# Pairing a head's backward retention scan with the next head's forward scan, with early chunks held in DRAM

## The chip, the core and the metric

The kernel runs on one core of a Trainium2 chip. The core has five engines that work side by side, each through its own queue in a fixed order: TensorE (PE in the profile; its weight loads are PEld) for matrix products and transposes, VectorE (DVE), ScalarE (ACT), GpSimd (POOL), and SyncE (SP), which here only issues DMA transfers. Engines wait for one another by semaphores. SBUF is the on-chip memory, PSUM the eight banks in which TensorE leaves its products, and DRAM the memory outside. The metric is the device time of one launch in microseconds; the times named before are the median of three runs.

## The reference

One block of a bidirectional encoder on 1024 tokens and 16 learned meta tokens that are put ahead of them, with 1024 channels, in float32. A normalised stream goes through one wide projection; two branches read parts of it, retention and windowed attention, and both are gated, projected and merged. The change concerns the retention branch and, through the order of work, the attention behind it.

```python
def _retention_direction(q, k, v, log_gamma, strict):
    ...
    decay = jnp.where(vis[None], jnp.exp(jnp.where(vis, rel, 0.0)[None] * log_gamma[:, None, None]), 0.0)
    s = jnp.einsum("bnihd,bnjhd->bnhij", q, k) * decay[None, None]
    inner = jnp.einsum("bnhij,bnjhv->bnihv", s, v)
    k_decay = jnp.exp((CHUNK - 1 - idx)[:, None] * log_gamma[None, :])
    kv = jnp.einsum("bnjhd,bnjhv->bnhdv", k * k_decay[None, None, :, :, None], v)
    chunk_decay = jnp.exp(CHUNK * log_gamma)[None, :, None, None]

    def step(state, kv_c):
        return chunk_decay * state + kv_c, state

    _, s_prev = lax.scan(step, jnp.zeros((B, H, DK, DV), jnp.float32), jnp.moveaxis(kv, 1, 0))
    ...
    cross = jnp.einsum("bnihd,bnhdv->bnihv", q * q_decay[None, None, :, :, None], s_prev)
    return (inner + cross).reshape(B, L, H, DV)

def _bidirectional_retention(q, k, v, log_gamma_f, log_gamma_b):
    fwd = _retention_direction(q, k, v, log_gamma_f, False)
    flip = lambda t: jnp.flip(t, axis=1)
    bwd = flip(_retention_direction(flip(q), flip(k), flip(v), log_gamma_b, True))
    return fwd + bwd
```

There are four retention heads of key size 128 and value size 256, and eight chunks of 128 tokens, with a short chunk 0 for the meta tokens. The sum of the two directions is normalised over each head's 256 values before it goes on. Attention has eight heads in two groups; each block of 128 queries sees itself, its two neighbours and the meta keys, with a sink logit in the softmax.

## The kernel before

Each float32 product is made of three float32r matmuls (`mm3`, lines 69 to 71): the operands are split into a rounded high part and the rest, and high times high, low times high and high times low are added up. The high part is made by a copy on ScalarE or GpSimd (`pool_hi`, line 74), the low part by a subtraction on VectorE (`dve_lo`, line 77). So every operand that changes costs two small instructions on other engines, ahead of the matmul.

PSUM has eight banks in four tags: three for projections (`pj`), two for transposes and scores (`p1`), two for state increments and attention scores (`p2`), and one (`p3`) for the output products of both scans and of attention.

The stages, in the order of time: a start, in which the first projection and the row norms are made; retention, head by head, from about 33 us; the values of attention (`gen_av`, tile `pav`); attention by four pairs of heads, from about 357 us; and from about 589 us the gates and the three big products, which the diff leaves alone.

`retention(h, fill)` treats one head. Its forward part runs over chunks 0 to 8. `stage1(c)` projects the values of chunk c (`pv`), transposes the keys and makes the scores in one bank (`tr`, lines 466 and 468), scales the keys for both directions (`kh`, `kl`) and applies the decay table to the scores (`sd`). `stage2(c)` makes the inner and the cross product in the `p3` bank (`pa`), adds both into the output chunk `op` (lines 506 and 507), makes the state increments of both directions (`pkv`), updates the forward state (`Sf`) and splits it, and keeps the backward increment in `kvb` (line 523). All eight `op` and all seven `kvb` stay in SBUF until the backward part needs them.

The backward part runs over chunks 8 to 1. For each it updates the state (`Sb`, line 572) and splits it, makes the cross product in `p3` (`pb`), adds it to `op` (line 579), takes mean and variance (lines 583 to 585), normalises the chunk before (line 587) and, for the chunk two before, transposes it (`finish`, `to`, line 555), copies it to `ost` with a scale (line 560), and stores two chunks at a time to `oTr_d`. The last two chunks of a head are finished inside the next head's forward part (`pend`).

Between the steps of the backward part, `fill(KT)` takes a portion of a generator of other projections, eight groups of matmuls: queries and keys of the next retention head (`gen_qk`, tiles `pk` and `pq`) for heads 0 to 2, and for head 3 attention's keys (`gen_ak`, `pak`), half the first pair's queries (`gen_aq`, `paq`) and one gate (`gen_gate(7)`, `pgt`). A projection of queries is 24 matmuls of 512 columns a tile and is evacuated by two VectorE products (`rope_evac`, lines 159 and 160) and two adding transfers of GpSimd. The order in the queues is set when the program is built: a scheduler places instructions by their priority and readiness, `issue_after` ties some behind others, and it draws filler ahead where the main work is not ready. So the built queues need not stand in the order of the source.

Attention of a pair (`attention(hp, fill)`) has three stages for each block n: scores of two heads (`ps`), mask and maximum in one VectorE instruction (line 1203), exponential, and a scaling on GpSimd; transposes of the probabilities (`pt`) with their splits (`pal`, `pbl`, `pm`); and the product with the values (`po`, in `p3`). `FILL` gives the portions of filler behind each block: for pair 0 the second half of its own queries, then the first half of the next pair's, and so on. Beside pair 0, `sums_of_x` loads x in 16 tiles (`xs`, line 664), scales them on ScalarE (line 669), subtracts them on VectorE (line 671) and stores the differences, which the big products use later.

Of the kernel before, what the change touches and what calls it, by code (L numbers as in the profile page):

```python
# [14 lines left out]
NM = 16  # L15
# [23 lines left out]
def block_kernel(ctx: ExitStack, tc: tile.TileContext, xT, x, w_in, w_rb, w_ab, w_out, vecs, dec, sink,  # L39
# [22 lines left out]

    xs_d = {n: dram.tile([4, P, 512], F32, tag=f"xs{n}", name=f"xs{n}") for n in ("T1", "T2", "T3", "T4")}
# [104 lines left out]
    tabt = ra.tile([P, 3 * P + 5], F32, name="tabt")  # L168
    idx = tabt[:, 3 * P:3 * P + 5]
    mask = ra.tile([P, MW], F32, name="mask")  # L170
# [44 lines left out]
    def decay_table(hs):  # L215
        for h in hs:
            t = ra.tile([P, P], F32, tag="dd", bufs=2, name=f"dd{h}")
            nc.vector.tensor_scalar(t, tabt[:, 2 * P:3 * P], lg[:, 4 + h:5 + h], None, op0=ALU.mult)
            nc.vector.scalar_tensor_tensor(t, tabt[:, P:2 * P], lg[:, h:h + 1], t, op0=ALU.mult, op1=ALU.add)
            nc.scalar.activation(DT[:, h], t, AF.Exp)  # L220
# [17 lines left out]
    with tc.tile_pool(name="setup", bufs=1, reuse_waits="tile") as st:  # L238
# [35 lines left out]
        nc.sync.dma_start(tabt[:, 0:3 * P], tab[:, MW:MW + 3 * P])  # L274
# [155 lines left out]
    pend = []  # L430

    def retention(h, fill):
        q, kt = qk[h]
        qh, ql = [], []
        for i in range(2):
            a = rp.tile([P, 512], R, tag="qh", bufs=2, name=f"qh{h}_{i}")
            b = rp.tile([P, 512], R, tag="ql", bufs=2, name=f"ql{h}_{i}")
# [5 lines left out]
        vmeta = rp.tile([NM, 256], F32, tag="vmeta", bufs=2, name=f"vmeta{h}")  # L443
        st1 = {}
        state = {"f": None, "b": None}
        pins = []

        def qs(ts, c):
            return ts[(c - 1) // 4][:, P * ((c - 1) % 4):P * ((c - 1) % 4) + P]
# [8 lines left out]
        def stage1(c):  # L458
            n = NM if c == 0 else P
            pv = first.pop(0) if first else projT(wv, c, f"pv{h}_{c}", vmeta)  # L460
            vh = rp.tile([P, 256], R, tag="vh", bufs=4, name=f"vh{h}_{c}")
            vl = rp.tile([P, 256], R, tag="vl", bufs=4, name=f"vl{h}_{c}")
            state["v"] = nc.scalar.copy(vh[0:n], pv[0:n, 0:256]).ins
# [27 lines left out]
        def split_state(sr_, nm):  # L491
            a = rp.tile([P, 256], R, tag="Sh", bufs=2, name=f"Sh{nm}")
            b = rp.tile([P, 256], R, tag="Sl", bufs=2, name=f"Sl{nm}")
            state["S"] = pool_hi(a, sr_)
            dve_lo(b, sr_, a)
            return a, b

        def stage2(c):
            n, vh, vl, kd, s = st1.pop(c)
            if c > 0:  # L500
# [4 lines left out]
                o = op[c - 1]  # L505
                nc.scalar.activation(o, pa[:, 0:256], AF.Copy, scale=rcol[:, c:c + 1])
                nc.vector.scalar_tensor_tensor(o, pa[:, 256:512], qdf(h, c), o, op0=ALU.mult, op1=ALU.add)
            if kd:
                pk = p2(f"pkv{h}_{c}")
            if "f" in kd:  # L510
                a, b = kd["f"]
                mm3(pk[:, 0:256], a[0:n], b[0:n], vh[0:n], vl[0:n], True, True)
                new = rp.tile([P, 256], F32, tag="S", bufs=2, name=f"Sf{h}_{c}")
                if c == 0:
                    nc.vector.tensor_copy(new, pk[:, 0:256])
                else:
                    nc.vector.scalar_tensor_tensor(new, state["f"], cdf(h), pk[:, 0:256], op0=ALU.mult, op1=ALU.add)
# [11 lines left out]
        for c in range(9):  # L529
            if c < 8:  # L530
                stage1(c + 1)
            if c == 1:
                while pend:
                    pend.pop(0)()
# [893 lines left out]
```

## Time and profile before

| | |
|---|---|
| median of 3 runs | 1093.3 us (1090.18 to 1094.16) |
| the profiled execution | 1094.51 us, of it 1092.7 us span |
| mean granted TensorE clock | 0.995 |
| DRAM read, written | 105.89 MB, 52.43 MB |
| idle time of TensorE in the span | 1092.7 - 1068.1 = 24.6 us |

The page of the profile gives the busy time of each engine; the span in 40 slices; the DMA queues; the chain of work that ended last, followed back from the end; the costliest groups of instructions with the idle time before them; and the DMA issues. Besides, the trace can be asked for the busy time of each engine in chosen stretches of time (with the clock granted to TensorE, DMA share and GB/s), for the groups in such a stretch, and for the single instructions in order of time. Matmuls overlap in TensorE's pipeline, so that the duration of one in a row (about 0.28 us for 256 columns) is longer than the distance to the next.

### The profile page before, as it was taken

The numbers are of one execution on the slowest core, as the hardware profiler recorded it, in microseconds if no ns is written. First come the engines' busy times: TensorE is split into PE (matmuls) and PEld (weight loads), VectorE is DVE, ScalarE is ACT, GpSimd is POOL, SyncE is SP. The second block draws the span as 40 slices with busy tenths as digits, with TensorE's granted clock in tenths as the row PEclk, the third lists the DMA queues.
The fourth block names the chain that finished last, engine by engine and source line by source line (L and its number), as shares of the span: only waits on it lengthen the run. The fifth ranks groups of instructions, "written<-read, shape, count | busy, mean of one in ns | idle before, by whom it ended". The sixth has DMA issues, their size and how long they took to land.

```text
span 1092.7 us, 17365 instructions
## 1 busy us (share of the span) xinstructions
PE 1068.1 (98%) x5975; PEld 922.5 (84%) x5975; DVE 827.4 (76%) x1816; ACT 490.0 (45%) x1132; POOL 265.7 (24%) x394
## 2 busy tenths in 40 slices
PE   8999999999999999999999999999999999999996
PEld 7899999998989889888887778888888788787885
DVE  7785767867946977777557875988889899767765
ACT  7241432413314455635657544454456546433442
POOL 3444334343422555464220000000000000010032
PEclk9999999998999999999999999999999999999999
DMA  7333122231324994243115654779874655789363
GB/s 288 78 86 71 58 42 78 68 69 39 88 59 162 313 269 120 64 98 87 49 40 192 222 204 142 243 246 321 263 285 141 218 201 198 235 209 335 112 115 78
DMA packets 83480, 168.95 MB, mean 155 GB/s; under 512 B 9664, under 2 KB 24512, under 8 KB 82624
## 3 DMA queue, kind: packets, MB, share of 16 engines
q1 hardware_dynamic: 71824, 151.78, 40.5%
q0 software_dynamic: 11136, 15.79, 9.7%
q8 instruction: 47, 0.77, 0.3%
q14 instruction: 41, 0.34, 0.1%
q10 hardware_dynamic: 432, 0.28, 0.1%
HBM read 105.89 MB, written 52.43 MB: 145 GB/s over the span
## 4 chain that ended last, share of the span: by engine, by line
PE 86%; DVE 6%; DMA 4%; ACT 2%; issue 2%; POOL 0%; SPq 0%; DVEq 0%; POOLq 0%; ACTq 0%
PE bz L70 6%; PE bz L71 6%; PE bz L69 6%; PE pv L69 3%; PE paq L70 3%; PE paq L71 3%; PE paq L69 3%; PE pv L70 3%; PE pv L71 3%; PE bo L70 2%; PE bo L69 2%; PE bo L71 2%; PE br L70 2%; PE br L71 2%; PE br L69 2%; PE ba L70 2%
## 5 line engine op out<-in xcount | busy, mean ns | idle before, releaser
L1054 POOL DMA_DIRECT2D mx_d<-c1a x4 | 3.5, 883 | 397.3 <-DVE c1a L1045 397.3
L70 PE MATMUL bz<-big,llz 128*128 128x512 f32 x208 | 82.4, 396 | 0.2 <-DVE llz L77 0.2
L69 PE MATMUL bz<-big,lhz 128*128 128x512 f32 x208 | 81.2, 396 | 0.6 <-ACT lhz L775 0.6
L71 PE MATMUL bz<-big,lhz 128*128 128x512 f32 x208 | 81.7, 394 | 0.0
L69 PE MATMUL pv<-wh,big 128*128 128x256 f32 x256 | 73.4, 287 | 0.7 <-DVE m_qk L160 0.7
L70 PE MATMUL pv<-wh,big 128*128 128x256 f32 x256 | 73.1, 286 | 0.0
L71 PE MATMUL pv<-wl,big 128*128 128x256 f32 x256 | 73.1, 285 | 0.0
L69 PE MATMUL bz<-T,lhz 128*128 128x512 f32 x156 | 61.7, 396 | 0.5 <-ACT u2z L850 0.5
L70 PE MATMUL bz<-T,llz 128*128 128x512 f32 x156 | 61.5, 394 | 0.0
L71 PE MATMUL bz<-T,lhz 128*128 128x512 f32 x156 | 61.4, 394 | 0.0
L1217 POOL TENSOR_SCALAR p<-p,den 128x400 f32<-128x400 f32 (+1 forms) x60 | 44.3, 897 | 43.5 <-DVE den L1211 29.1
L70 PE MATMUL paq<-big,wl 128*128 128x512 f32 x128 | 51.2, 400 | 0.0
L69 PE MATMUL paq<-big,wh 128*128 128x512 f32 x128 | 50.7, 396 | 0.0
L71 PE MATMUL paq<-big,wh 128*128 128x512 f32 x128 | 50.5, 395 | 0.0
L69 PEld LDWEIGHTS pv<-wh,big 128*128 128x128 f32 x256 | 48.9, 191 | 1.1 <-DVE m_qk L160 1.0
L74 POOL TENSOR_SCALAR wh<-wr 128x1024 fp32r<-128x1024 f32 x32 | 39.9, 1335 | 36.8 <-PE pav L70 12.7
L70 PEld LDWEIGHTS pv<-wh,big 128*128 128x128 f32 x256 | 48.8, 190 | 0.1
L71 PEld LDWEIGHTS pv<-wl,big 128*128 128x128 f32 x256 | 48.8, 191 | 0.0
L77 DVE TENSOR_TENSOR wl<-wr,wh 128x1024 fp32r<-128x1024 f32 x34 | 42.9, 1265 | 6.9 <-POOL wh L74 6.9
L69 PEld LDWEIGHTS bz<-big,lhz 128*128 128x128 f32 x208 | 39.0, 188 | 10.7 <-ACT lhz L775 1.5
L70 PEld LDWEIGHTS bz<-big,llz 128*128 128x128 f32 x208 | 39.1, 188 | 9.4 <-DVE llz L77 0.4
L71 PEld LDWEIGHTS bz<-big,lhz 128*128 128x128 f32 x208 | 39.1, 188 | 9.0
(614 smaller groups left out, 3669.2 us busy)
## 6 DMA issues: line engine op xcount, KB each, us to landing
wr<-in_w_in_dram SPq DMA_DIRECT2D x35, 512.0 KB, 4.2
wrz<-in_w_in_dram SPq DMA_DIRECT2D x28, 512.0 KB, 5.4
tg<-tg_d SPq DMA_DIRECT2D x32, 256.0 KB, 5.3
T<-preT SPq DMA_DIRECT2D x6, 1024.0 KB, 7.5
oTr_d<-ost SPq DMA_DIRECT2D x16, 256.0 KB, 2.1
aq<-m_aq POOLq DMA_DIRECT2D x32, 128.0 KB, 4.2
xs<-in_xT_dram SPq DMA_DIRECT2D x16, 256.0 KB, 5.6
xsT<-xs SPq DMA_DIRECT2D x16, 256.0 KB, 5.2
```

Of the source, the lines that this page charges most:

```text
L69: nc.tensor.matmul(o, ah, bh, start=first, stop=False, **kw)
L70: nc.tensor.matmul(o, al, bh, start=False, stop=False, **kw)
L71: return nc.tensor.matmul(o, ah, bl, start=False, stop=last, **kw).ins
L74: return nc.gpsimd.tensor_scalar(o, i, 1.0, 1.0, op0=ALU.mult, op1=ALU.mult).ins
L77: return nc.vector.tensor_tensor(o, i, hi.bitcast(F32), ALU.subtract).ins
L1054: nc.gpsimd.dma_start(d, to, accum_op=ALU.add)
L1217: nc.gpsimd.tensor_scalar(pt[e_][:, 0:wid], pt[e_][:, 0:wid], den[:, e_:e_ + 1], 1.0, op0=ALU.mult, op1=ALU.mult)
```

## The change

The two parts of a head become two generators, `forward(h)` and `backward(h)`, each of which gives up control after every chunk. A loop over five rounds runs the forward chunks of head h, the backward chunks of head h-1 and a portion of filler in turn. Chunks 1 to 5 (`LATE = 6`) of the forward output and increments 2 to 5 go to two sets of DRAM tiles, `op_d` and `kv_d`, right after they are made; the backward part loads them back two chunks ahead into `opl` and `kvl`, with two buffers each. Chunks 6 to 8 stay in SBUF. So that both scans fit, other buffers are cut: `m1` 4 to 3, `vh` and `vl` 4 to 3, `ost` and `vmeta` 2 to 1, `dd` joins the tag of `rw`, and the forward state is updated in place in one buffer; the split queries get four buffers where they had two, and the split states get tags of their own for each direction.

Beside that, the V weights of head h+1 are loaded in round h's seventh step, the fillers of the last rounds are shuffled (both halves of the first pair's queries, then the keys; the gate goes to attention's pair 0), the rope tables are scaled in round 2, the identity is loaded straight from DRAM, and the mask lies in attention's pool and is loaded when retention's pool is closed, ahead of the loads of x. Numbers of matmuls, transposes and other engine instructions stay as they were, but for three small VectorE instructions less; SP issues 73 more transfers.

```diff
+    op_d, kv_d = ([dram.tile([NB, P, 256], F32, tag=f"{n}{i}", name=f"{n}_d{i}") for i in range(2)] for n in ("op", "kv"))
...
-        m1 = ra.tile([P, 512], F32, tag="m1", bufs=4, name=f"m1_{nm}")
+        m1 = ra.tile([P, 512], F32, tag="m1", bufs=3, name=f"m1_{nm}")
...
+        nc.sync.dma_start(ident, tab[:, MW:MW + P])
+        nc.sync.dma_start(tabt[:, 0:2 * P], tab[:, MW + P:MW + 3 * P])
...
-    nc.vector.tensor_copy(ident, tabt[:, 0:P])
     nc.sync.dma_start(sinkc, sink.partition_broadcast(P))
-    nc.sync.dma_start(mask, tab[:, 0:MW])
...
-    def retention(h, fill):
+    scans = {}
+    LATE = 6
...
+    def split_state(sr_, nm):
+        a = rp.tile([P, 256], R, tag="Sh" + nm[0], bufs=2, name=f"Sh{nm}")
+        b = rp.tile([P, 256], R, tag="Sl" + nm[0], bufs=2, name=f"Sl{nm}")
...
+    def forward(h):
...
-        wv = wv0 if h == 0 else load_w(w_in, U_V + h)
-        kvb = [None] + [rp.tile([P, 256], F32, tag="kvb", bufs=NB - 1, name=f"kvb{h}_{c}") for c in range(1, NB)]
-        op = [rp.tile([P, 256], F32, tag="op", bufs=NB, name=f"op{h}_{c}") for c in range(NB)]
+        kvb, op = {}, {}
+        scans[h] = qh, ql, kvb, op
+        wv = wvs.pop(h)
...
-                o = op[c - 1]
+                kept = c >= LATE
+                o = op[c] = rp.tile([P, 256], F32, tag=f"op{int(kept)}", bufs=2 + kept, name=f"op{h}_{c}")
                 nc.scalar.activation(o, pa[:, 0:256], AF.Copy, scale=rcol[:, c:c + 1])
                 nc.vector.scalar_tensor_tensor(o, pa[:, 256:512], qdf(h, c), o, op0=ALU.mult, op1=ALU.add)
+                if not kept:
+                    nc.sync.dma_start(op_d[h % 2][c - 1], o)
...
-                nc.scalar.copy(kvb[c - 1], pk[:, 256:512])
+                kept = c >= LATE
+                t = kvb[c] = rp.tile([P, 256], F32, tag=f"kvb{int(kept)}", bufs=2 + kept, name=f"kvb{h}_{c}")
+                nc.scalar.copy(t, pk[:, 256:512])
+                if not kept:
+                    nc.sync.dma_start(kv_d[h % 2][c - 1], t)
...
             stage2(c)
-
-
+            yield
+
+    def backward(h):
+
+        qh, ql, kvb, op = scans.pop(h)
...
-                ost[0] = rp.tile([P, 2, 256], F32, tag="ost", bufs=2, name=f"ost{h}_{c}")
+                ost[0] = rp.tile([P, 2, 256], F32, tag="ost", bufs=1, name=f"ost{h}_{c}")
...
         for c in range(NB, 0, -1):
-            o = op[c - 1]
+            if 2 < c <= LATE + 1:
+                l = op[c - 2] = rp.tile([P, 256], F32, tag="opl", bufs=2, name=f"opl{h}_{c}")
+                nc.sync.dma_start(l, op_d[h % 2][c - 3])
+                if c > 3:
+                    l = kvb[c - 2] = rp.tile([P, 256], F32, tag="kvl", bufs=2, name=f"kvl{h}_{c}")
+                    nc.sync.dma_start(l, kv_d[h % 2][c - 3])
+            o = op[c]
...
-            if c < 8:
-                with ExitStack() as behind:
-                    for p in pins:
-                        behind.enter_context(tc.issue_after(p))
-                    fill(KT)
             if c < NB - 1:
                 finish(c + 2)
+            yield
         state["n", 1]()
-        pend.extend([lambda: finish(2), lambda: finish(1)])
+        finish(2)
+        finish(1)
+        yield
...
-    for h in range(NH):
-        fill, drain = filler([*([gen_qk(h + 1)] if h < 3 else [gen_ak(0), gen_aq(0, 0), gen_gate(7)])])
...
-        with tc.issue_after(rotated):
-            retention(h, fill)
+    wvs = {0: wv0}
+    with tc.issue_after(rotated):
+        for h in range(NH + 1):
+            fill, drain = filler([gen_qk(h + 1)] if h < 3 else [gen_aq(0, 0), gen_aq(0, 1)] if h == 3 else [gen_ak(0)])
+            f, b = forward(h) if h < NH else iter(()), backward(h - 1) if h else iter(())
+            for i in range(NB + 1):
+                next(f, None)
+                next(b, None)
+                fill(KT)
+                if h == 2 and i > 6:
+                    turn_factors(*PIECES[2 * i - 14])
+                    turn_factors(*PIECES[2 * i - 13])
+                if h < 3 and i == 6:
+                    wvs[h + 1] = load_w(w_in, U_V + h + 1)
             drain()
-    while pend:
-        pend.pop(0)()
+            for _ in b:
+                pass
...
+    mask = ap.tile([P, MW], F32, name="mask")
+    nc.sync.dma_start(mask, tab[:, 0:MW])
...
-        l = [gen_aq(hp, 1)]
+        l = [gen_aq(hp, 1)] if hp else [gen_gate(7)]
```

More of the change, by code (lines that the diff above doesn't have):

```diff
@@ L460, in stage1 @@
             pv = first.pop(0) if first else projT(wv, c, f"pv{h}_{c}", vmeta)
[L461 to L463 removed]
+            vh = rp.tile([P, 256], R, tag="vh", bufs=3, name=f"vh{h}_{c}")
+            vl = rp.tile([P, 256], R, tag="vl", bufs=3, name=f"vl{h}_{c}")
+            nc.scalar.copy(vh[0:n], pv[0:n, 0:256])
             state["vl"] = dve_lo(vl[0:n], pv[0:n, 0:256], vh[0:n])
@@ L511, in stage2 @@
                 a, b = kd["f"]
+                new = state["f"]
                 mm3(pk[:, 0:256], a[0:n], b[0:n], vh[0:n], vl[0:n], True, True)
-                new = rp.tile([P, 256], F32, tag="S", bufs=2, name=f"Sf{h}_{c}")
                 if c == 0:
+                    new = rp.tile([P, 256], F32, tag="S", bufs=1, name=f"Sf{h}")
                     nc.vector.tensor_copy(new, pk[:, 0:256])
                 else:
-                    nc.vector.scalar_tensor_tensor(new, state["f"], cdf(h), pk[:, 0:256], op0=ALU.mult, op1=ALU.add)
+                    nc.vector.scalar_tensor_tensor(new, new, cdf(h), pk[:, 0:256], op0=ALU.mult, op1=ALU.add)
                 state["f"] = new
@@ L531, in retention @@
                 stage1(c + 1)
-            if c == 1:
-                while pend:
-                    pend.pop(0)()
-            if h == 0 and c == 4:
-                pins.extend((state["v"], state["vl"], state["S"]))
-            if h == NH - 1 and 1 < c < 6:
-                with tc.issue_after(state["vl"]):
-                    turn_factors(*PIECES[c - 2])
             if h < NH - 1 and c == 4:
```

56 lines of the change are left out of this document (23 added, 33 removed).

## The prediction, made before the changed kernel ran

> **What bounds the kernel now.** I read the page first: its busy table, its clock row and its chain of waits.
>
> ```profile
> span 1092.7 us, 17365 instructions
> PE 1068.1 (98%) x5975; PEld 922.5 (84%) x5975; DVE 827.4 (76%) x1816; ACT 490.0 (45%) x1132; POOL 265.7 (24%) x394
> PEclk9999999998999999999999999999999999999999
> PE 86%; DVE 6%; DMA 4%; ACT 2%; issue 2%; POOL 0%; SPq 0%; DVEq 0%; POOLq 0%; ACTq 0%
> ```
>
> TensorE is busy for 98% of the span and carries 86% of the chain. The change issues exactly the matmuls and transposes of before, so it can only win time in which TensorE idles (24.6 us in the span) or runs slowly, and the clock row has one dip, in the tenth slice. The next view, busy time by stretches, was cut at the stages: heads 0 to 3 of retention from 36 to 340 us, and attention's first two head pairs from 357 to 462. Columns: stretch, length, busy time (instructions) of PE, PEld, DVE, ACT and POOL, granted clock, DMA share, GB/s.
>
> ```profile
> 36.00:100.00 64.00, 63.87 (x489) 60.95 (x490) 43.74 (x113) 17.48 (x50) 33.15 (x41) 1.00 0.33 70
> 100.00:175.00 75.00, 74.16 (x572) 70.46 (x571) 56.77 (x159) 25.68 (x80) 31.20 (x47) 1.00 0.28 70
> 175.00:250.00 75.00, 73.98 (x575) 70.73 (x574) 54.59 (x149) 23.43 (x71) 29.36 (x45) 1.00 0.24 58
> 250.00:276.00 26.00, 23.41 (x167) 22.09 (x167) 20.01 (x59) 10.38 (x32) 8.48 (x13) 0.87 0.16 57
> 276.00:340.00 64.00, 64.00 (x406) 57.33 (x405) 44.64 (x113) 16.91 (x49) 24.43 (x35) 1.00 0.31 84
> 357.00:462.00 105.00, 104.44 (x637) 93.34 (x635) 83.98 (x227) 55.99 (x165) 54.12 (x87) 1.00 0.65 192
> ```
>
> Retention is already dense: over the first five stretches TensorE idles 0.13 + 0.84 + 1.02 + 2.59 + 0 = 4.6 us. The idle time stands where one head's backward scan ends and the next head's forward scan begins, and the worst turn, from head 2 to 3, looks like this (timeline of TensorE, the bracket is idle time before the row and its releaser; then the same place in stretches of 2 us):
>
> ```profile
> 256.77 0.36 PE L69 MATMUL pb<-Shb,qh 128*128 128x256 f32 x1 [0.45 <-DVE op L579]
> 258.42 0.41 PE L555 MATMUL to<-ident,op 128*128 128x128 f32 x2 [1.05 <-DVE op L587]
> 259.54 0.48 PE L466 MATMUL tr<-ident,kr 128*128 128x128 f32 x1 [0.61 <-ACT ost L560]
> ...
> 256.00:258.00 2.00, 0.92 (x6) 0.50 (x4) 1.69 (x6) 0.63 (x2) 0.66 (x2) 1.00 0.42 139
> 258.00:260.00 2.00, 0.97 (x5) 0.72 (x6) 1.97 (x7) 0.86 (x3) 1.04 (x3) 0.80 0.00 0
> 260.00:262.00 2.00, 2.00 (x10) 1.55 (x8) 1.62 (x6) 0.74 (x2) 0.27 (x2) 0.50 0.39 131
> 264.00:266.00 2.00, 2.00 (x11) 2.00 (x11) 1.36 (x5) 0.51 (x2) 0.40 (x1) 0.50 0.00 0
> ```
>
> The last chunks have no filler left: scan product, VectorE update, norm, transpose and ScalarE copy follow one another. After about 4 us at under half load the granted clock falls to 0.50 for some 6 us. Over the 26 us the clock is 0.87, which costs 26 x 0.13 = 3.4 us.
>
> **The change part by part.** (1) *Interleaving.* Head h-1's backward chunk stands beside head h's forward chunk and a filler portion, so the turns have other work. If all of it is won: 4.6 + 3.4 = **-8.0 us**. A gain beyond that could lie only in bubbles inside rows counted as busy; zero would remain if the stalls just moved. I take -8.0, since the built program's TensorE queue shows projection matmuls between the scan products at every turn.
>
> (2) *Early chunks through DRAM.* Per head, five forward outputs and four state increments are stored and read back: 18 transfers a head, 72 in all, of 128 KB. The nearest rows, and those of the backward recurrence (transfers: KB, us to landing; then groups of instructions from 36 to 340 us: busy us, mean ns, idle time before):
>
> ```profile
> oTr_d<-ost SPq DMA_DIRECT2D x16, 256.0 KB, 2.1
> ...
> L583 DVE BATCH_NORM_STATS2 bs<-op 128x6 f32<-128x256 f32 x31 | 13.0, 420 | 0.3
> L579 DVE SCALAR_TENSOR_TENSOR op<-pb,qd,op 128x256 f32<-128x256 f32 x27 | 13.0, 481 | 18.4 <-PE pb L71 18.0
> L587 DVE TENSOR_SCALAR op<-op,mv,rs 128x256 f32<-128x256 f32 x30 | 12.6, 418 | 0.2
> L584 DVE BATCH_NORM_AGGREGATE mv<-bs 128x2 f32<-128x6 f32 x31 | 5.4, 173 | 0.3
> L585 DVE TENSOR_SCALAR rs<-mv 128x1 f32<-128x1 f32 x31 | 4.7, 150 | 0.9
> ```
>
> The 72 transfers themselves are cheap: the DMA share in retention is 0.16 to 0.33. The wait they add is not. Reloaded outputs have two buffers, so the load for chunk 3 waits until chunk 5 is transposed, 2 until 4, 1 until 3: a recurrence of update 481 + statistics 420 + 173 + 150 + norm 418 ns + transposes about 0.4 us + a transfer of 2.1 us = 4.1 us a chunk, for three chunks of four heads. VectorE runs in order, so behind a waiting update stand the next forward chunk's splits; and the one bank of the third PSUM tag, now shared by both scans in turn, stays held, so the next output product waits too. SP's queue is held as well by a load that waits for its buffer, and what stands behind it are stores and the next V weights, which are due a whole scan later. Against that, a chunk of a head lasts 75 / 9 = 8.3 us in the rows above, twice the recurrence. Bounds: 0, and 12 x 2.1 = 25 us if every such load were waited for in full. The recurrence is half a chunk's time, so I stay near the lower end with one load in twelve: **+2.1 us**.
>
> (3) *Attention's first pairs lose their filler.* In the built program TensorE's queue has six more query projections (144 matmuls of 512 columns) ahead of attention's first score product than before; the queues agree again at the third pair. Rows for the pace of such a matmul (a stretch with little else), for their VectorE evacuation and the subtractions of x (groups from 357 to 462 us), and for a stretch in which attention has no filler now:
>
> ```profile
> 700.00:725.00 25.00, 25.00 (x109) 20.27 (x108) 20.29 (x33) 10.69 (x19) 0.00 (x0) 1.00 0.79 263
> ...
> L159 DVE TENSOR_TENSOR aq<-paq,cr 128x512 f32<-128x512 f32 x9 | 6.1, 682 | 1.2 <-PE paq L71 1.2
> L160 DVE TENSOR_TENSOR m_aq<-paq,sr 128x512 f32<-128x512 f32 x8 | 5.4, 679 | 0.0
> L671 DVE TENSOR_TENSOR xs<-xs,xs 128x512 f32<-128x512 f32 x12 | 9.1, 760 | 1.6 <-ACT xs L669 1.5
> ...
> 454.00:460.00 6.00, 6.00 (x44) 5.54 (x43) 4.44 (x15) 3.88 (x12) 1.86 (x5) 1.00 0.13 44
> 460.00:466.00 6.00, 4.46 (x27) 3.33 (x26) 5.91 (x27) 5.12 (x23) 1.46 (x5) 1.00 0.00 0
> ```
>
> 109 wide matmuls in 25.00 us are 229 ns each, so 144 take 33.0 us out of the stretch from 357 to 462: TensorE has 104.44 - 33.0 = 71.4 us there. VectorE loses six evacuations of 0.682 + 0.679 us, 8.2 in all, and gains the four subtractions of x (of sixteen) that lay ahead of this stretch, 4 x 0.760 = 3.0: 83.98 - 8.2 + 3.0 = 78.8 us. VectorE becomes the longer engine. With its best share (5.91 of 6.00) it needs 80.0 us, 8.6 more than TensorE, of which 0.56 us was lost already: upper bound +8.0. From below: 454 to 466 is bare attention; its first 6 us lose nothing, then VectorE is full and TensorE does 4.46 of 6. The built queue has 174 attention instructions in a row without a filler. At 6.00 / 44 us each that is 23.7 us of TensorE; beyond the first 6, 17.7 x 1.54 / 4.46 = 6.1 us, less the 1.54 lost now: +4.6. I take the middle, **+6.3 us**.
>
> (4) *x and the mask are loaded later.* Both stand behind the last output store of retention on SP's queue; between that store's transposes and the first scores the built queue has 33 wide matmuls, 33 x 229 ns = 7.6 us:
>
> ```profile
> xs<-in_xT_dram SPq DMA_DIRECT2D x16, 256.0 KB, 5.6
> ```
>
> One such transfer takes 5.6 us, with ScalarE's scaling behind it and then subtractions that stand ahead of the softmax on VectorE. Bounds 0 and 5.6; most of it lies beside those 7.6 us, so **+1.0 us**. A pause here could also trip the clock for another 3.4 us.
>
> The identity's direct load, buffers moved from one tag to another, the accumulation of the state in place and the meta rows' single buffer I cost at nothing: their waits end under projections in a retention that is at full clock and 99% busy outside the turns; uncovered, each would show one 0.48 us update or copy a chunk.
>
> On the clock, 256 to 260 us shows 2.1 us of idle time in pieces, none over 1.05, and then half speed. [...]
>
> Sum on the profiled execution's own time (1094.5 us, span 1092.7 with 1.8 around it): 1094.5 - 8.0 + 2.1 + 6.3 + 1.0 = 1095.9. That execution lies 1.2 us above the median of the runs shown, 1093.3, so for a median I say 1094.7, written **1095**.
>
> **The rivals.** *A, the turns are won and attention keeps up.* VectorE could use pauses ahead of attention and run a pair late without TensorE noticing; in the stretch before it, it is busy for 6.99 of 17 us:
>
> ```profile
> 340.00:357.00 17.00, 17.00 (x147) 17.00 (x146) 6.99 (x20) 9.09 (x22) 2.78 (x6) 1.00 0.58 194
> ```
>
> Against it: VectorE's 5.91 of 6.00 where filler is missing. Only (1) and a little of the rest remain: 1093.3 - 8.0 = 1085.
>
> *B, VectorE's queue sets the first two pairs.* From the first score product, VectorE's queue is full with subtractions that wait for x, and it decides as soon as its work there exceeds TensorE's: 8.0 + 5.6 + 3.4 for a tripped clock, against a gain of 8.0 - 2.1. 1093.3 + 17.0 - 5.9 = 1104, slower. For it speaks the sum of (3); against it that the first 6 us of bare attention lost nothing now.
>
> *C, the trip through DRAM sets the backward scan.* Half of the twelve loads waited for in full, 12.6 us, decisive from the point where a chunk's other work falls under 4.1 us: with (3) and (4), 1093.3 - 8.0 + 12.6 + 7.3 = 1105. Head 3's backward scan, with no forward scan beside it, is the likeliest place; against it, the 8.3 us of a chunk in the rest.
>
> *D, the change does not do what it says.* The engines' queues are static, and the new partners of a chunk could wait on one another as the turns do now; then the 8.0 us stay and (3) is paid: 1093.3 + 6.3 = 1100.
>
> **How the numbers follow.** Forecast 0.34, A 0.28, B 0.24, C 0.09, D 0.05. About 0.5%, 5.5 us, is what a measurement of this kernel can tell from no change, so faster means under 1087.8 and slower above 1098.8. A goes to faster but for its upper edge, 0.27; B, C, D and the upper edge of the forecast (its own range 1090 to 1101, from the bounds of (3) and (4) and from zero for (2)) to slower, 0.41; 0.32 stays. The range takes in A's and B's times and a little more on the side of the unbounded waits: 1084 to 1108.
>
> **What would show it.** Step 1: no clock under 1.00 between 36 and 340 us, and idle time of TensorE there under 2 us. Step 2: rows of TensorE waiting for an update of the third bank, led back to a reload; more than 3 us in all makes it C. Step 3: between the first pair's start and the third's, VectorE above 95% and TensorE under 92%; TensorE at 98% makes it A. Step 4: score or transpose rows that wait for x or for the softmax in the first 10 us of attention. Wrong altogether would be a time outside 1084 to 1108, or most of the difference arising behind 590 us, in the gate and output products that the change does not touch.

## The result, and the profile after

The changed kernel takes 1107.2 us (median of four runs, 1103.5 to 1108.4) against 1093.7 before: the ratio is 1.0125, with a 95% interval of 1.0093 to 1.0157. It is slower, clear of the noise, by less than 2%. The profiled execution is the fastest of the four, 1103.5 us with a span of 1101.7, which is 9.0 us over the profiled execution of before. Where the other runs lose 3.7 us more is not in any trace. The ratios leave out two launches: one of the last experiment's kernel took 1752.6 us, at a mean clock of 0.56, and one of the kernel before took 5366.8 us.

The page of the changed kernel, in its busy table, clock row and chain of waits:

```profile
span 1101.7 us, 17528 instructions
PE 1071.1 (97%) x5975; PEld 920.1 (84%) x5975; DVE 825.6 (75%) x1815; ACT 488.9 (44%) x1132; POOL 263.0 (24%) x394
PEclk9999999999999999999999999999999999999999
PE 85%; DMA 5%; DVE 4%; issue 2%; POOL 1%; ACT 1%; SPq 0%; DVEq 0%; POOLq 0%; ACTq 0%
```

TensorE idles 30.6 us instead of 24.6 and is busy for 1071.1 us instead of 1068.1. To see where, both spans are cut at the same events: the first value product, the first score product, the first score of attention's third pair, and the first gate product behind attention. The rows of before (columns as in the prediction):

```profile
32.70:357.10 324.40, 318.69 (x2361) 300.14 (x2359) 230.14 (x615) 103.57 (x305) 129.41 (x185) 0.99 0.30 78
357.10:462.00 104.90, 104.33 (x636) 93.24 (x634) 83.88 (x227) 55.89 (x165) 54.12 (x87) 1.00 0.65 192
462.00:588.70 126.70, 123.77 (x701) 107.53 (x701) 83.94 (x251) 68.50 (x203) 45.39 (x81) 1.00 0.30 84
```

and of the changed kernel:

```profile
32.00:391.50 359.50, 352.26 (x2507) 326.38 (x2506) 239.33 (x624) 103.27 (x303) 138.92 (x198) 1.00 0.39 102
391.50:478.10 86.60, 77.82 (x497) 66.94 (x496) 73.35 (x225) 57.71 (x172) 41.84 (x76) 1.00 0.65 212
478.10:599.20 121.10, 120.81 (x691) 105.24 (x689) 81.06 (x238) 65.13 (x194) 45.46 (x81) 1.00 0.27 72
```

Six projections (33.0 us by the prediction's pace) have moved from attention into the first stretch. So retention takes 359.5 - 324.4 - 33.0 = 2.1 us longer, and attention takes 207.7 us where it took 231.6, so that 33.0 - 23.9 = 9.1 us are lost there. Of these, 5.6 us are idle time (9.1 us, where it was 3.5); the other 3.5 us lie in rows counted as busy, and no trace here takes them apart. The start is 0.7 us and the products behind 599 us are 1.5 us shorter: -0.7 + 2.1 + 9.1 - 1.5 = 9.0.

The first turns are indeed filled: from 36 to 276 us TensorE idles 1.5 us. But in the fourth round the filler is used up, and this is the view of 2 us stretches at the point where it ends:

```profile
286.00:288.00 2.00, 1.44 (x13) 1.23 (x11) 1.64 (x2) 0.22 (x1) 1.63 (x2) 1.00 0.00 0
288.00:290.00 2.00, 0.93 (x7) 0.93 (x8) 2.00 (x4) 0.37 (x1) 0.88 (x2) 1.00 0.62 231
290.00:292.00 2.00, 0.61 (x5) 0.41 (x4) 2.00 (x6) 0.77 (x2) 0.72 (x1) 1.00 0.30 76
292.00:294.00 2.00, 2.00 (x10) 2.00 (x10) 1.02 (x5) 0.00 (x0) 0.64 (x1) 0.50 0.92 301
```

The timeline of the same place, VectorE's queue first and then the two instructions of TensorE that waited for it:

```profile
286.36 1.23 DVE L79 TENSOR_TENSOR wl<-wr,wh 128x1024 fp32r<-128x1024 f32 x1 [0.47 <-POOL wh L76]
287.50 1.12 DVE L79 TENSOR_TENSOR sl<-sd,sh 128x128 fp32r<-128x128 f32 x1
288.55 0.47 DVE L589 SCALAR_TENSOR_TENSOR op<-pb,qd,op 128x256 f32<-128x256 f32 x1
289.33 1.21 DVE L79 TENSOR_TENSOR wl<-wr,wh 128x1024 fp32r<-128x1024 f32 x1
291.33 0.40 DVE L79 TENSOR_TENSOR vl<-pv,vh 128x256 fp32r<-128x256 f32 x1
...
289.07 0.39 PE L71 MATMUL pa<-vh,sh 128*128 128x256 f32 x1 [1.63 <-DVE op L589]
291.79 0.42 PE L71 MATMUL pak<-big,wh 128*128 128x272 f32 x1 [1.39 <-DVE vl L79]
```

VectorE splits the weights of attention's keys (`wl`) in the middle of two scans' small operations. The backward update (`op`, line 589) releases the one `p3` bank, for which the forward product `pa` waits; the value split (`vl`) releases the projection bank, for which the keys wait. TensorE idles 3.0 us of 6, and then runs at half clock for 3.4 us, which costs 1.7. Until 340 us the idle time adds up to 4.5 us, as much as the turns cost before.

In attention's first two pairs TensorE waits for every engine in turn (waits of TensorE from 391.5 to 480 us: total us, times, longest):

```profile
PE pt L1248 <- POOL p L1238: 2.4, 3, 1.4
PE po L71 <- ACT oa L1284: 1.9, 4, 0.9
PE ps L71 <- DVE den L1231: 1.3, 1, 1.3
PE po L71 <- ACT pbh L1270: 1.1, 2, 0.7
PE po L71 <- ACT pah L1258: 1.0, 2, 0.7
```

Over these 86.6 us VectorE is busy for 73.35, 85%. But that is an average, and attention's start looks otherwise (stretches of 5 us, and three rows of VectorE's queue):

```profile
395.00:400.00 5.00, 3.70 (x19) 2.90 (x17) 4.96 (x13) 3.40 (x10) 1.21 (x2) 1.00 1.03 403
400.00:405.00 5.00, 3.57 (x17) 2.44 (x18) 5.00 (x14) 2.48 (x8) 2.93 (x6) 1.00 1.06 406
...
396.56 2.70 DVE L679 TENSOR_TENSOR xs<-xs,xs 128x512 f32<-128x512 f32 x4
399.18 0.62 DVE L1224 CUSTOM_DVE_ANT_0 p<-ps,mask,nsink 128x400 f32<-128x400 f32 x1
399.74 0.15 DVE L1231 TENSOR_TENSOR den<-den,es 128x2 f32<-128x2 f32 x1
```

From 395 to 405 us VectorE is full, and 2.7 of the 8.8 us of idle time lie there: the softmax's sums (`den`) stand behind four subtractions of x. The other 6 us lie in short pauses between 415 and 478 us, in stretches of 5 us in which VectorE is busy for 75 to 97%; whether its queue or the length of a block's chain sets them is not shown.

### The profile page after: what moved, and what is told of

It reads as the page before. It is cut to its first block, busy times and chain, and to the rows that moved or that the text cites. A ratio compares the mean times of both kernels' runs of the same rounds, so it can differ in the third digit from the quotient of the medians.

```text
span 1101.7 us, 17528 instructions
## 1 busy us (share of the span) xinstructions
PE 1071.1 (97%) x5975; PEld 920.1 (84%) x5975; DVE 825.6 (75%) x1815; ACT 488.9 (44%) x1132; POOL 263.0 (24%) x394
## 4 chain that ended last, share of the span: by engine, by line
PE 85%; DMA 5%; DVE 4%; issue 2%; POOL 1%; ACT 1%; SPq 0%; DVEq 0%; POOLq 0%; ACTq 0%
PE bz L72 8%; PE bz L73 8%; PE bz L71 8%; PE bo L72 2%; PE br L72 2%; PE bo L71 2%; PE bo L73 2%; PE br L71 2%; PE br L73 2%; PE pv L71 2%; PE pv L73 2%; PE pv L72 2%; PE ba L72 2%; PE pgt L72 2%; PE pgt L73 2%; PE pgt L71 2%
## 5 line engine op out<-in xcount | busy, mean ns | idle before, releaser
L1238 POOL TENSOR_SCALAR p<-p,den 128x400 f32<-128x400 f32 (+1 forms) x60 | 40.1, 760 | 47.0 <-DVE den L1232 38.8
```

The source lines that it names most:

```text
L1238: nc.gpsimd.tensor_scalar(pt[e_][:, 0:wid], pt[e_][:, 0:wid], den[:, e_:e_ + 1], 1.0, op0=ALU.mult, op1=ALU.mult)
```

## The experiments

The theories as they stood before the first runs: (1) attention loses because the filler was drawn ahead of it; (2) the trip through DRAM and the shared bank set the loss; (3) VectorE's bursts in rounds with two scans do. Theory 4 was added after the first four runs: head 3's backward scan has no partner, its reload chain has to be covered, and the filler that covers it is what attention lacks. All times are medians (of four runs; of twelve for e_last), and the ratios are to the kernel before on the same chip.

| run | us | ratio, 95% interval |
|---|---|---|
| changed kernel | 1107.2 | 1.0125, 1.0093 to 1.0157 |
| e_pin | 1114.5 | 1.0183, 1.0162 to 1.0204 |
| e_pinr | 1103.7 | 1.0086, 1.0069 to 1.0103 |
| e_both | 1116.0 | 1.0209, 1.0178 to 1.0239 |
| e_lo | 1101.8 | 1.0068, 1.0050 to 1.0085 |
| e_h3pin | 1107.9 | 1.0134, 1.0113 to 1.0155 |
| e_serial | 1127.8 | 1.0316, 1.0296 to 1.0335 |
| e_serial4 | 1102.4 | 1.0081, 1.0057 to 1.0105 |
| e_fill | 1100.5 | 1.0073, 1.0050 to 1.0096 |
| e_xs | 1107.8 | 1.0136, 1.0114 to 1.0159 |
| e_best | 1107.8 | 1.0134, 1.0104 to 1.0164 |
| e_best1 | 1110.9 | 1.0153, 1.0123 to 1.0183 |
| e_last | 1090.8 | 0.9974, 0.9962 to 0.9986 |

**Filler back into attention (e_pin).**

```diff
             if hp < 3 or n < NB - 2:
-                fill(FILL[hp][n])
+                with tc.issue_after(scored[-1]) if hp == 0 else ExitStack():
+                    fill(FILL[hp][n])
```

> The changed kernel, but the filler portions of attention's pair 0 are tied behind that block's score products on TensorE, so that the six query projections stand among the pair's blocks again instead of ahead of them. Theory 1 (attention without filler is set by VectorE; +9 us there in the profiles): the stretch from the first score product to the third pair loses its idle time, and 7 to 9 us of the 13.5 come back, less 1 to 3 us where the end of retention has less filler: 1099 to 1102 us. Theory 2 (the trip through DRAM and the shared bank set the loss): within 2 us of the changed kernel, 1105 to 1109. Theory 3 (a VectorE burst in the turn to head 3, with its half clock, is the larger part): 1103 to 1106.

It took 1114.5 us, which none of the theories expected. From 392 to 500 us TensorE is busy all but 0.35 us, as theory 1 says; the changed kernel idles 9.1 us in its attention. But more is lost ahead of it than gained there, from 344 us to attention's first products at 367 us and, still at half clock, until 378 us. Three stretches of 4 us and the one from 392:

```profile
352.00:356.00 4.00, 0.90 (x4) 0.54 (x3) 1.89 (x5) 0.88 (x3) 0.41 (x1) 0.50 0.41 139
356.00:360.00 4.00, 1.14 (x5) 0.47 (x3) 1.02 (x5) 0.63 (x2) 0.58 (x1) 0.50 0.11 33
360.00:364.00 4.00, 1.64 (x5) 1.00 (x5) 1.05 (x4) 0.63 (x2) 0.58 (x1) 0.50 0.20 68
...
392.00:500.00 108.00, 107.65 (x657) 95.90 (x655) 78.75 (x222) 54.05 (x167) 51.28 (x85) 1.00 0.52 144
```

This is head 3's backward scan with nothing beside it. One chunk of it in the timeline:

```profile
354.87 0.48 DVE L589 SCALAR_TENSOR_TENSOR opl<-pb,qd,opl 128x256 f32<-128x256 f32 x1
355.38 0.43 DVE L593 BATCH_NORM_STATS2 bs<-opl 128x6 f32<-128x256 f32 x1
356.13 0.40 DVE L597 TENSOR_SCALAR opl<-opl,mv,rs 128x256 f32<-128x256 f32 x1
356.68 0.66 PE L560 MATMUL to<-ident,opl 128*128 128x128 f32 x2 [0.20 <-DVE opl L597]
357.37 0.32 SPq L574 DMA_DIRECT2D opl<-op_d  x1
359.45 0.48 DVE L589 SCALAR_TENSOR_TENSOR opl<-pb,qd,opl 128x256 f32<-128x256 f32 x1 [2.91 <-DMA opl<-op_d]
360.08 0.55 PE L71 MATMUL pb<-Shb,qh 128*128 128x256 f32 x1 [2.73 <-DVE opl L589]
```

From update to update it is 4.6 us, at half clock: update, statistics, norm of the chunk before, transposition, which frees the buffer, reload, next update; and the next `pb` waits for the bank. This is the recurrence that the prediction put at 4.1 us and held to be covered. In the changed kernel it is: 161 filler matmuls (96 of the gate, 65 of queries) and 42 value matmuls lie between the scan's first product and its last transposition, counted in the trace; before the change it was 60 (all of the gate) and 111. So theory 4 was formed.

**Filler of the fourth round tied to its chunks (e_pinr).**

```diff
+                with tc.issue_after(mark[0]) if h == 3 else ExitStack():
+                    fill(KT)
```

(`mark[0]` is the score matmul of the forward scan's current chunk; the old line goes.)

> The changed kernel, but the filler of the fourth round (first pair's queries) is tied behind the current chunk's score matmul of head 3's forward scan, so that it isn't used up in the round before. Theory 3 (the turn to head 3 runs dry at 287 to 292 us, 4.5 us idle and 1.7 us of half clock): idle time of TensorE from 276 to 340 us falls under 2 us, and the time to 1101 to 1104. Theory 1: the turn may get better, but attention still loses its 9 us: no lower than 1101. Theory 2: 1105 to 1109, and the idle time moves to another chunk that waits for a reload.

```profile
232.00:258.00 26.00, 19.34 (x75) 14.13 (x75) 15.03 (x48) 8.43 (x26) 5.05 (x11) 0.67 0.23 73
276.00:340.00 64.00, 63.80 (x500) 61.47 (x498) 48.70 (x127) 20.94 (x62) 28.15 (x39) 1.00 0.43 118
```

The place at 287 us is healed, as theory 3 said, and the end of the round before is now the dry one: 6.7 us idle and a clock of 0.67. The median is 3.5 us better, the two profiled executions have the same span (1101.6 and 1101.7). Here the loss moved to the stretch that the filler left.

**Both ties (e_both).**

> Both ties together. Theories 1 and 3 add up: 13.5 - 9 - 5 leaves about the time of before or a little less, 1090 to 1096. Theory 2: 1103 or more.

1116.0 us: the effects don't add up to a gain. Head 3's scan lies bare as in e_pin, and the third round as in e_pinr. Theories 1 and 3 in their simple form, each place with a price of its own, fall here.

**Weight splits off VectorE (e_lo).** The low parts of the weights of attention's first keys and of the values are made by GpSimd.

```diff
-            dve_lo(l, raw, h)
+            if spare:
+                nc.gpsimd.tensor_tensor(l, raw, h.bitcast(F32), ALU.subtract)
+            else:
+                dve_lo(l, raw, h)
```

> The changed kernel, but the low parts of the weights of attention's keys (group 0) and values are subtracted on GpSimd instead of VectorE (four subtractions of 128x1024). Theory 3 (VectorE's burst of weight splits, 1.2 us each, holds up the scans' small operations at 287 and 312 us): TensorE's idle time from 276 to 340 us falls from 4.5 to under 2 us, no half clock, 1101 to 1104. If it is the order of the queues alone or the reloads (theory 2) that hold the scans: 1105 to 1109, or more if GpSimd is late with the weights.

```profile
276.00:340.00 64.00, 61.47 (x511) 60.21 (x510) 45.45 (x133) 22.50 (x67) 31.83 (x43) 1.00 0.39 108
400.00:406.00 6.00, 5.04 (x15) 3.92 (x16) 5.97 (x18) 3.78 (x10) 4.50 (x8) 0.51 1.05 400
```

1101.8 us, 5.4 better in the median (2.0 between the profiled executions) and within what theory 3 gave. The idle time from 276 to 340 us falls from 4.5 to 2.5 us, not under 2, and the half clock at 292 us is gone; another stands at attention's start. So VectorE's burst is a part of it, about half of that idle time.

**Head 3's reloads in four buffers (e_h3pin, on top of e_pin).**

```diff
-                l = op[c - 2] = rp.tile([P, 256], F32, tag="opl", bufs=2, name=f"opl{h}_{c}")
+                l = op[c - 2] = rp.tile([P, 256], F32, tag="op0" if h == NH - 1 and 3 < c < 6 else "opl", bufs=2,
+                                       name=f"opl{h}_{c}")
```

> The kernel with the filler of pair 0 tied to its blocks (1114.5 us), and in head 3's backward scan alone the reloads of chunks 2 and 3 go into the two buffers of the early forward outputs, which are free by then, so that no reload of head 3 waits for a transposition. Theory 4 (head 3's backward scan has no partner, and its chain of update, norm, transposition and reload takes 4.6 us a chunk, 355.5 to 360.1 us in the last profile): the last chunks come 2 to 3 us apart, the half clock lasts less than 30 us, and the time falls to 1103 to 1109. If the chain within a chunk (update, statistics, norm) sets the pace without the reload: 1112 to 1116.

1107.9 us instead of 1114.5. VectorE's waits for reloaded outputs, 5.9 us in e_pin's last scan, are gone, the last products start at 349.0, 350.7 and 353.6 us, and the first score product comes 9 us earlier (358.1 instead of 367.1). Theory 4 holds for the chain; the scan is still bare, and the clock still halved for part of it (0.80 granted on average from 340 to 392 us).

**No interleaving (e_serial).** Trip through DRAM, cut buffers and late mask as in the change; each backward scan behind its own forward scan, filler shares as before.

```diff
-            f, b = forward(h) if h < NH else iter(()), backward(h - 1) if h else iter(())
-            for i in range(NB + 1):
-                next(f, None)
-                next(b, None)
-                fill(KT)
+            for _ in forward(h):
+                pass
+            b = backward(h)
+            for _ in range(NB + 1):
+                next(b, None)
+                fill(KT)
```

(The loads of the V weights and the scaling of the rope tables move along.)

> The trip through DRAM, the cut buffers and the late mask of the changed kernel, but each head's backward scan runs behind its own forward scan again, with the filler where it was before the change. Theory 2 (the trip and the shared buffers cost time by themselves): 1098 or more, with waits for reloads in every head. Theory 4 (the trip costs only where nothing covers it): within 4 us of before, 1092 to 1098, since each backward scan has its filler; the idle time at the turns is as before, 4 to 6 us.

1127.8 us, 34.3 over before, so theory 2's words were the right ones here: the trip and the cut buffers do cost time by themselves. The waits of TensorE from 36 to 392 us name the chain again:

```profile
PE to L560 <- DVE opl L597: 14.9, 12, 4.0
PE pb L71 <- DVE opl L589: 14.4, 6, 2.8
```

Filler beside the scans, in the shares of before, didn't cover it in the first three heads: each has about 10 us of these waits and 17 us at half clock (the granted clock is 0.93 from 36 to 276 us and 0.87 from 276 to 340). Head 3's scan, with 96 matmuls of the gate and 149 of the values beside it, is covered:

```profile
344.00:396.60 52.60, 52.60 (x348) 47.55 (x347) 23.69 (x68) 13.07 (x35) 12.88 (x22) 1.00 0.35 104
```

**The same with four reload buffers in every head (e_serial4).** The edit of e_h3pin without its condition on the head.

> The run without interleaving (1127.8 us), but in every head's backward scan the reloads of chunks 2 and 3 go into the two buffers of the early forward outputs, so that no reload waits for a transposition. If the recurrence through the two reload buffers makes most of the 34 us over before (theory 4; TensorE waited 14.9 us for norms and 14.4 us for updates of reloaded chunks there): three to four heads gain some 6 us each and the three half clocks of 17 us get shorter: 1095 to 1108. If it is the other cut buffers (one store tile, three value tiles, states of their own): 1118 to 1128.

1102.4 us: 25 of the 34 us were the recurrence through two buffers. The waits for updates of reloaded chunks fall from 14.4 to 0.9 us and those for norms from 14.9 to 5.0:

```profile
PE to L560 <- DVE opl L598: 5.0, 7, 1.4
PE tr L474 <- ACT ost L565: 4.8, 3, 1.7
PE pb L71 <- DVE opl L590: 0.9, 2, 0.5
```

The remaining 9 us (0.81%) weren't taken apart. A part is `ost`, which has one buffer now: ScalarE's copies into it wait 21.2 us in all until it has been stored (none did before the change), and the next head's key transposes wait 4.8 us for such a copy (1.8 before).

**Interleaving with the old shares of filler (e_fill).**

```diff
-            fill, drain = filler([gen_qk(h + 1)] if h < 3 else [gen_aq(0, 0), gen_aq(0, 1)] if h == 3 else [gen_ak(0)])
+            fill, drain = filler([gen_qk(h + 1)] if h < 3 else [] if h == 3 else [gen_ak(0), gen_aq(0, 0), gen_gate(7)])
...
-        l = [gen_aq(hp, 1)] if hp else [gen_gate(7)]
+        l = [gen_aq(hp, 1)]
```

> The changed kernel with the interleaving kept, but the filler shared out as before the change: none in the fourth round, attention's keys, half of the first pair's queries and the gate in the last one, and the other half of the queries in pair 0. Theory 4 (the loss is where the filler went, not what the interleaving does at the turns): attention's idle time falls from 9 us to about 2, head 3's backward scan is as long as before the change (31 us), and the time is 1088 to 1096. Theory 3 (rounds with two scans are set by VectorE's bursts, and the more so without filler in the fourth): idle time and half clock in the fourth round grow, 1098 to 1106. Theory 1 alone: what attention gains is not lost elsewhere, 1096 to 1100.

```profile
242.00:246.00 4.00, 2.83 (x22) 2.60 (x22) 3.96 (x13) 1.22 (x3) 0.98 (x2) 1.00 0.02 4
246.00:250.00 4.00, 1.84 (x16) 1.63 (x14) 1.88 (x4) 0.63 (x2) 0.99 (x2) 1.00 0.29 98
310.00:330.00 20.00, 20.00 (x96) 16.51 (x96) 8.92 (x25) 4.32 (x11) 6.12 (x10) 1.00 0.45 105
```

1100.5 us, 27 better than e_serial with the same filler, buffers and trips: that is what interleaving is worth while reloads have two buffers. Without interleaving, e_serial4's four buffers do nearly as much (ratio 1.0081 against 1.0073), which suggests that most of these 27 us are cover for the recurrence. And e_fill is 7 better than the changed kernel (3.1 between the profiled executions), which differs from it in the shares of filler alone. Head 3's scan is covered (no idle time from 310 to 392 us), attention idles 3 us, and the third and fourth round lose 10 us between 236 and 310 us, where theory 3 expected a loss; theory 4's 1088 to 1096 was missed. It isn't VectorE's bursts alone: `pa` waits 3.2 us there for updates of reloaded chunks, that is for the bank that both scans share.

**x later (e_xs).** The call for the sums of x was moved from pair 0 to pair 2.

> The changed kernel, but the loads, scalings, subtractions and stores of x run beside attention's pair 2 instead of pair 0. Theory 1 in its form of the sum (VectorE's total work is the bound in the first two pairs): 16 subtractions of 0.69 us, 11 us, leave that stretch, and 5 to 8 us come back: 1099 to 1102. If each block's own chain (scores, exponential, scaling, transposes) is what TensorE waits for without filler: only the first blocks gain, 1104 to 1107.

Nothing follows from its 1107.8 us: the scheduler drew the work ahead again, and the subtractions ran from 391.8 to 417.1 us, where they had run from 390.7 to 415.3. So VectorE's load as the bound at attention's start, where it was full, has not been tested.

**Half of the gate, or most of it, beside head 3's scan (e_best, e_best1).** e_lo, four buffers for head 3, and the tie of e_pin from the third, or from the fifth, portion of filler on (`hp == 0 and n > 1`, `n > 3`).

> The changed kernel with three edits together: low parts of the weights of attention's keys and values on GpSimd, head 3's reloads in four buffers, and the filler of pair 0 tied behind its blocks' scores from the third portion on, so that about half of the gate (48 matmuls of 512 columns, 11 us) stays beside head 3's backward scan and four projections stay in pair 0, as before the change. Theory 4 with theories 1 and 3: the last scan's 12 us of idle time are covered, attention has none, the turn to head 3 has 2 us: 1085 to 1094. If filler is short in all (what one place gains, another loses): 1096 to 1102.

> The same, but tied from the fifth portion on: the whole gate (96 matmuls, 22 us) beside head 3's backward scan, two projections in pair 0. Theory 4: the scan is covered with some to spare, attention's pair 0 loses 2 to 4 us of it: 1088 to 1096, near the run with half of the gate. If filler is short in all: 1096 to 1102.

1107.8 and 1110.9 us, beyond either forecast. The trace of e_best1 has 72 of the gate's 96 matmuls ahead of the first score product, not the whole gate; from 364 to 380 us TensorE is busy for 8.0 of 16 us there, at a clock of 0.54. In e_best the scan is covered until 352 us, and now attention's start is bare:

```profile
356.00:360.00 4.00, 2.07 (x10) 1.11 (x9) 3.67 (x15) 1.05 (x4) 1.58 (x3) 0.85 0.49 164
364.00:368.00 4.00, 1.27 (x4) 0.95 (x4) 1.91 (x8) 0.67 (x4) 0.60 (x2) 0.50 0.80 207
372.00:376.00 4.00, 2.03 (x5) 1.02 (x5) 3.60 (x12) 4.00 (x10) 2.50 (x4) 0.50 1.05 395
```

The first scores, their softmax and transposes follow one another, the DMA is full with x, and half speed lasts from 359 to 390 us. That is step 4 of the prediction without its cover.

**Interleaving, old shares but for one, three reload buffers (e_last).** e_fill with half of the first pair's queries in the fourth round, e_lo's split, `opl` with three buffers (the room comes from `sd`, 3 to 2).

```diff
-... [] if h == 3 else [gen_ak(0), gen_aq(0, 0), gen_gate(7)])
+... [gen_aq(0, 0)] if h == 3 else [gen_ak(0), gen_gate(7)])
...
-                l = op[c - 2] = rp.tile([P, 256], F32, tag="opl", bufs=2, name=f"opl{h}_{c}")
+                l = op[c - 2] = rp.tile([P, 256], F32, tag="opl", bufs=3, name=f"opl{h}_{c}")
```

> Interleaving kept; the filler shared out as before the change, but for half of the first pair's queries (48 matmuls, 11 us), which go to the fourth round, where the run with the old shares lost 10 us between 236 and 310 us; three reload buffers instead of two in every head; low parts of the weights of attention's keys and values on GpSimd. The built queue then reaches attention's first score product and the second pair at the same places as before the change. Theory 4 (interleaving gains at the turns what it should as soon as the reload chain and the filler's shares don't take it back): attention's idle time as before, 1 to 2 us, the last scan covered, idle time from 36 to 340 us under 3 us: 1086 to 1093, faster than before. Theory 3 (rounds with two scans are limited by VectorE's bursts whatever fills them): 5 us or more of idle time and half clock in the third and fourth round stay: 1094 to 1100.

1090.8 us, ratio 0.9974 (0.9962 to 0.9986): faster than both kernels, by 0.26% over before. From attention's first score product to its third pair TensorE idles 1.0 us, where it was 0.6 before the change and 8.8 in the changed kernel:

```profile
360.80:465.80 105.00, 103.98 (x637) 93.24 (x636) 87.15 (x235) 61.07 (x175) 54.89 (x88) 1.00 0.68 209
```

Idle time from 36 to 340 us is 7.0 us in its trace, not under 3, so that half of the expectation failed; theory 3's 5 us in the third and fourth round are there nearly in full (4.4 us from 175 to 340 us), but the half clock is elsewhere: the granted clock is 0.97 from 36 to 100 us and 1.00 from 100 to 340. The profiled execution took 1094.1 us, 3.3 above the median; where the median gains its 3 us can't be read from it.

## Why the prediction was right in its direction, and where it failed

The forecast was 1095, 1.7 us over before, from a sum of four terms. The measured 1107.2 is 13.5 us over, outside the forecast's own 1090 to 1101, and inside 1084 to 1108 only because that range was drawn to take in the rivals. "Slower" was its likeliest outcome, at 0.41, but the forecast itself lay within the 5.5 us that it took for no change. So the direction was right with a sum that was wrong in its largest term. Held against the profiled execution (sum 1095.9, measured 1103.5), the terms stand so:

- **Step 1, -8.0 us, failed.** It took the gain in full because projections stand between the scan products in the built queue at every turn. At the first turns this came true (1.5 us of idle time from 36 to 276 us, no half clock). But the filler is finite, and in the fourth round, with two scans and no projection that is ready, TensorE lost 4.5 us of idle time and 1.7 us to the clock. Counted as the step counted it, from 36 to 340 us, that is 6.0 + 1.7 = 7.7 us, where it was 4.6 + 3.4 = 8.0: a gain of 0.3 us instead of 8.0. Together with step 2 the sum had -5.9 us for this stretch; it came out at +2.1, of which 2.4 us are in rows counted as busy, or idle outside these bounds, and stay open. The 8.0 us between the two are the main miss; steps 3 and 4 were 1.8 short, and 2.2 us came back at the start and behind attention, so the sum is 7.6 us off.
- **Step 2, +2.1 us.** Its recurrence was right: 4.1 us forecast, 4.6 measured. That it costs little while it is covered was right too: in the changed kernel no row of TensorE's waits from 36 to 392 us leads to an update of a reloaded chunk. What the step overlooked is the price of the cover: head 3's backward scan has no partner, and the scheduler covers it with the very filler that step 3 misses in attention. The two were booked as independent. e_pin shows that they are one account: with the filler back in attention, the scan costs more than attention gains. Uncovered in three heads, the recurrence costs 25 us (e_serial less e_serial4), as much as the step's upper bound for four.
- **Steps 3 and 4, +7.3 us, came out at +9.1.** That attention loses for want of filler is shown by e_pin, where TensorE idles 0.35 us from 392 to 500 us, and by e_fill (3.0 us). The mechanism was right in part: VectorE was to be above 95% over the whole stretch, and is at 85%; it is full only from 395 to 405 us, with 2.7 of the 8.8 us of idle time. In the rest TensorE waits for GpSimd, ScalarE and VectorE in turn. That this is the length of a block's chain is argued, not shown. TensorE's share, 77.82 of 86.6, is under the 92% that was named. Of step 4, scores that wait 1.3 us for the softmax's sums behind subtractions of x were found at 400 us.
- **Rivals.** A's condition (TensorE at 98% in the first pairs) didn't occur. B and C lie nearest to the result, with 1104 and 1105, but by luck. B's condition was that VectorE's work exceeds TensorE's in the first pairs; it is 73.35 against 77.82 us, and the clock didn't fall there. C needed more than 3 us of waits led back to reloads, and the changed kernel has none. C named head 3's backward scan as the likeliest place; it is, once the cover is gone. D, to which it gave 0.05, is nearest in its account: the 8.0 us of step 1 stay, in another place, and attention's loss is paid.
- The remaining difference is -1.5 us behind attention, in products that the change doesn't touch, and -0.7 us at the start, where the loads of the identity and the mask changed; neither was taken apart.

In ratios the whole change takes apart like this: the trip and the cut buffers alone +3.2% (+0.8% with four reload buffers), interleaving brings that to +0.7%, and the new shares of filler to +1.25%. With a third reload buffer and filler shared nearly as before, with weight splits on GpSimd, it is -0.26%. Which of these three makes the difference in the last run wasn't measured.

## What to carry to other kernels

Filler that covers a wait is a budget: before a cover is booked as free, ask which later stretch it is drawn from, and add both to one account. A tile that is reloaded two steps ahead into two buffers isn't ahead at all when its last reader is as late as here: the load waits for that reader, and the transfer becomes part of the chain (one update of e_pin waited 2.91 us for it). And when a scan is paired with its neighbour, look at the last one, which has no neighbour.

## What the runs showed of the hardware

The clock fell to half after broken idle time again: at 292 us in the changed kernel after 3.0 us of idle time in 6, of which no single wait was longer than 1.63 us. In the 4 us just ahead of the drop TensorE was busy for 1.54 us, and for 2.23 us in the 4 us ahead of the drop in the kernel before (255.2 to 259.2 us, a little over half, where the prediction says under half); but 1.64 of 4 us from 399 to 403 us in the changed kernel brought no drop (granted clock 1.00), so no threshold follows. Half speed lasted 3.4 us in the changed kernel (292.0 to 295.4 us), 6.8 us before (259.2 to 266.0) and, worked out from the granted clock at 0.50 for the halved part, about 50 us over the first three heads of e_serial (0.93 from 36 to 276 us, 0.87 from 276 to 340), 21 us in e_h3pin (0.80 from 340 to 392 us) and 31 us in e_pin (0.70 there).
